# Attention by pairs of heads with a feature-major result, and the squares of the residual moved from GpSimd to ScalarE and VectorE

## The chip, the cores and the metric

The kernel runs on one core of a Trainium2 chip. The metric is the device time of one execution in microseconds (us). Engines: PE is TensorE (matrix products; PEld its weight loads), DVE is VectorE, ACT is ScalarE, POOL is GpSimd, SP issues the loads.

## What is computed

A chain of blocks on 256 tokens of 1024 features, in f32: layer 0 (half a feed-forward, a Mamba-2 mixer, half a feed-forward, shared keys and values), layer 1 (half a feed-forward, windowed attention on the shared keys and values, half a feed-forward), then a block with two mixers and a layer of 16,384 experts. The change touches the attention of layer 1 and the norm at the entry of each block. From the reference:

```python
def rmsnorm(x, g):
    xf = x.astype(jnp.float32)
    y = xf * lax.rsqrt(jnp.mean(xf * xf, axis=-1, keepdims=True) + EPS)
    return (y * g.astype(jnp.float32)).astype(x.dtype)

# sliding_window_attention, one block of 128 queries; 16 query heads of 64, 2 key heads
        s = jnp.einsum('bqkrd,bskd->bkrqs', qk, kk).astype(jnp.float32) * scale + bias
        valid = in_window & ((bi > 0) | (kj >= blk))
        s = jnp.where(valid, s, -jnp.inf)
        m = jnp.maximum(jnp.max(s, axis=-1, keepdims=True), sink)
        p = jnp.exp(s - m)
        denom = jnp.sum(p, axis=-1, keepdims=True) + jnp.exp(sink - m)
        return jnp.einsum('bkrqs,bskd->bqkrd', (p / denom).astype(vk.dtype), vk)
```

## The kernel before

The residual `h` lies feature-major: 8 parts of 128 features by 256 tokens. Every large product is made of three: weights and inputs are each split into a high part that PE takes at full rate and a rest, and `mm3` (lines 153 to 155) adds low weight by high input, high by low and high by high. Weights arrive in groups of 8 blocks of 128 x 128; for each group ACT makes the high part (line 93) and DVE the rest (line 99).

Each block begins with `norm_in`: the gain is multiplied in and the part split, on ACT (line 181) and DVE (line 182), while `norm_sum` (lines 206 to 210) squares and adds the 8 parts on POOL; the scale per token, made from the sum, is put in after the products. The expert layer (`peer`) calls `norm_sum` itself and splits the parts into `uhi` and `ulo`. Eight entries of blocks do this: four feed-forward layers, Mamba, attention, the two mixers together, experts. In four of them the residual is updated part by part some 8 us apart (line 319, behind a feed-forward layer); in three, two parts at a time (lines 261 and 501); the first reads the input.

Attention: `project` makes the queries of four heads (two groups of weights each), their squares by POOL, the sums per head by PE (line 674) and the factors on DVE. `attn_head` handles one head: scores by PE (lines 609 and 610, the head's 64 features on one half of the partitions), scale, bias and maximum on DVE (613 to 616), the exponential on ACT (619), three transposes by PE (623), a copy by ACT (628), and three products with the values (630 to 632) that leave 64 columns per head in a token-major bank `po`. After eight heads `tail` divides by the denominator (708), transposes back to feature-major (716) and splits for the output projection (719 and 720), which runs in two halves of four pairs (`proj_half`, line 261 adds it to `h`). Projections, output projection and heads are woven step by step, and a scheduler that works from estimates sets the final order on each engine. All of PSUM is one pool of 8 banks (`K.bank`). `K.warm` issues dummy products of zeros.

Of the kernel before, what the change touches and what calls it, by code (L numbers as in the profile page):

```python
# [7 lines left out]
F32 = mybir.dt.float32  # L8
# [4 lines left out]
AF = mybir.ActivationFunctionType  # L13
# [4 lines left out]
T = 256  # L18
# [30 lines left out]
class Ctx:  # L49
# [145 lines left out]

    def bcast(self, rt, st, c, n, out):

        self.nc.tensor.matmul(out, rt[:, st, c:c + 1].to_broadcast([128, n]), self.ident, start=True, stop=True)

    def norm_sum(self, h):  # L200

        nc = self.nc
        acc = self.tmp.tile([128, T], F32, name="ssq", tag="ssq")
        for k in range(KD):
            if k == 0:
                nc.gpsimd.tensor_mul(acc, h[:, k], h[:, k])
            else:
                s = self.tmp.tile([128, T], F32, name="sq", tag="sq", bufs=2)
                nc.gpsimd.tensor_mul(s, h[:, k], h[:, k])
                nc.gpsimd.tensor_add(acc, acc, s)  # L210
            yield acc

    def norm_in(self, h, g):

        nc = self.nc
        hi = self.xp.tile([128, KD, T], F32R, name="xhi", tag="xhi")
        lo = self.xp.tile([128, KD, T], F32R, name="xlo", tag="xlo")
        for k, acc in enumerate(self.norm_sum(h)):
            self.split_x(h, g, hi, lo, k)

        def scale(between=None, tok=False):
            rt = self.rs_tok(acc, self.ones[:, 0:1], 1, 1.0 / 1024, EPS, "n")
            if tok:
                return rt
            if between is not None:
                between()
            ps = self.bank()
            for st in range(2):
                self.bcast(rt, st, 0, 128, ps[:, st * 128:(st + 1) * 128])
            rs = self.tmp.tile([128, T], F32, name="rs", tag="rs", bufs=2)  # L230
            nc.scalar.activation(rs, ps[:, :T], AF.Copy)
            return rs, rt

        return hi, lo, scale
# [408 lines left out]
def attention(K, h, P, kv, w_q, w_o, bias, pool):  # L643
# [8 lines left out]
    den = pool.tile([128, 16, 2], F32, name="den")  # L652
    sc = pool.tile([128, 16, 2], F32, name="qsc")
    u = pool.tile([128, 16, 2], F32, name="qu")
    otok = pool.tile([128, 2, 1024], F32, name="otok")
    ohi = pool.tile([128, 8, T], F32R, name="ohi")
    olo = pool.tile([128, 8, T], F32R, name="olo")
    blk = K.stream(w_q)
# [24 lines left out]
            V.tensor_scalar(sv[:, st], sv[:, st], rt[:, st], 0.125, OP.mult, OP.mult)  # L683
        scaled.append(m)

    def head(hd):
        kvh, p0, c = hd // 8, 64 * (hd % 2), (hd % 8) * 64
        while hd // 4 not in scaled:
            yield
        if hd % 8 == 0:  # L690
            po[kvh] = [K.bank("po") for _ in range(2)]
        s = pool.tile([128, 384], F32, name="as", tag="as", bufs=4)
        sT = pool.tile([128, 384], F32, name="asT", tag="asT", bufs=3)
        yield from attn_head(K, s, qT[p0:p0 + 64, hd // 2], kd[p0:p0 + 64, kvh], vtok[:, :, kvh * 64:kvh * 64 + 64],
                             sc[:, hd], (bias[:, hd, 128:256], bias[:, hd]), nsink[:, hd:hd + 1], nm[:, hd], den[:, hd],
                             [p[:, c:c + 64] for p in po[kvh]], sT, hd % 4 < 0)
        if hd % 8 == 7:
            tails.append(tail(kvh))

    def tail(g):  # L700
        gs = slice(8 * g, 8 * g + 8)
        V.tensor_tensor(u[:, gs], nm[:, gs], nsink[:, gs].unsqueeze(2).to_broadcast([128, 8, 2]), OP.subtract)
        A.activation(u[:, gs], u[:, gs], AF.Exp)
        yield
        V.tensor_add(den[:, gs], den[:, gs], u[:, gs])
        V.reciprocal(den[:, gs], den[:, gs])
        for st in range(2):
            V.tensor_tensor(otok[:, st, g * 512:(g + 1) * 512].rearrange("p (a b) -> p a b", b=64),
                            po[g][st].rearrange("p (a b) -> p a b", b=64),
                            den[:, gs, st].unsqueeze(2).to_broadcast([128, 8, 64]), OP.mult)  # L710
        for _ in range(1):
            yield
        for st in range(2):
            ps = K.bank()
            for i in range(4):
                TE.transpose(ps[:, i * 128:(i + 1) * 128], otok[:, st, (4 * g + i) * 128:(4 * g + i + 1) * 128], K.ident)
            dst = (slice(None), slice(g * 4, g * 4 + 4), slice(st * 128, st * 128 + 128))
            pr = ps.rearrange("p (a b) -> p a b", b=128)
            A.activation(ohi[dst], pr, AF.Copy)
            V.tensor_sub(olo[dst], pr, ohi[dst].bitcast(F32))  # L720
            yield
        done.append(g)

    def heads():
        for _ in weave((head(hd) for hd in range(16)), 1):
            if tails and next(tails[0], tails) is tails:
                tails.pop(0)
            yield
        while tails:
            if next(tails[0], tails) is tails:  # L730
                tails.pop(0)
            yield

    def fill():
        for m in range(1, 4):
# [4 lines left out]
                yield  # L740
            yield from K.proj_half(blk, g, ohi[:, 4 * g:4 * g + 4], olo[:, 4 * g:4 * g + 4], h)

    scaled, tails, done, po = [], [], [], {}
    p0 = project(0)
    for _ in range(2):
        next(p0)
    rt = scale(tok=True)
    run((p0, 1), (fill(), 1), (heads(), 1))


EM05 = float(np.exp(-0.5))
# [1210 lines left out]
```

## Time and profile before

| | |
|---|---|
| median of 3 runs | 2160.61 us (2148.82 to 2167.58) |
| the profiled execution | 2161.79 us |
| its span in the trace | 2160.0 us |
| mean granted clock of PE | 0.982 |
| busy: PE, DVE, ACT, POOL | 97%, 72%, 50%, 14% |

The span is what the trace covers, 1.8 us less than the execution's own time. Busy PE time is not PE at its peak: products overlap, so the cost of one is read from the starts of two that follow each other, and the same products take twice the time where the granted clock stands at its lower level. The attention stage lies at about 804 to 904 us of the span, its heads from 816.8; the entries of the blocks lie at 0, 204, 404, 606, 804, 897, 1101 and 1308 us.

### The profile page before, as it was taken

To read this page: it belongs to the slowest core of one execution; us is meant where nothing else is said; L and a number is where in the kernel's file an instruction comes from. 1 tells how busy PE (TensorE), PEld (TensorE's weight loads), DVE (VectorE), ACT (ScalarE), POOL (GpSimd) and SP (SyncE) were. 2 spreads that over 40 slices of the span, in tenths; PEclk is the share of its full clock that TensorE was granted. 3 is DMA by queue.
4 is the path that set the end of the run, shared out by engine and by line. 5 is a ranking of instruction groups with operands and counts; after the bars stand their busy time and mean duration, and the time that the engine had idled before them with its cause. 6 is when DMAs were issued, how large, how long until landed. Compare 5 with 4: busy or idle time off the path is not lost. (4 is left out here: it accounts for less than half of the span.)

```text
span 2160.0 us, 40955 instructions
## 1 busy us (share of the span) xinstructions
PE 2103.4 (97%) x16522; PEld 1981.3 (92%) x16522; DVE 1556.5 (72%) x2862; ACT 1070.0 (50%) x1810; POOL 295.3 (14%) x246
## 2 busy tenths in 40 slices
PE   8999999999999999999998898999999999999999
PEld 8999998999999998899987778999999998888887
DVE  6665978776576656576569778997788886656565
ACT  4444678454454444454443445553444444454544
POOL 2002000200100020200154316751000000000000
PEclk9999999999999997899999999999999999999999
DMA  6555443676555552355542206542444444555554
GB/s 210 186 187 178 157 149 98 174 203 205 181 181 179 188 181 79 118 186 186 186 147 74 94 23 218 167 168 85 159 161 158 157 158 168 191 188 192 187 193 148
DMA packets 98282, 348.16 MB, mean 161 GB/s; under 512 B 11083, under 2 KB 13996, under 8 KB 97836
## 3 DMA queue, kind: packets, MB, share of 16 engines
q1 hardware_dynamic: 98092, 345.54, 48.4%
q8 instruction: 130, 2.13, 0.4%
q14 instruction: 60, 0.49, 0.1%
HBM read 344.05 MB, written 1.44 MB: 160 GB/s over the span
## 5 line engine op out<-in xcount | busy, mean ns | idle before, releaser
L99 DVE TENSOR_TENSOR wlo<-wraw,whi 128x1024 fp32r<-128x1024 f32 x597 | 743.0, 1246 | 304.6 <-ACT whi L93 302.5
L93 ACT ACTIVATE whi<-wraw 128x1024 fp32r<-128x1024 f32 x644 | 677.1, 1053 | 402.0 <-PE ps L155 218.7
L153 PE MATMUL ps<-xhi,wlo 128*128 128x256 f32 x1960 | 561.8, 287 | 15.8 <-DVE wlo L124 7.7
L154 PE MATMUL ps<-xlo,whi 128*128 128x256 f32 x1960 | 557.0, 284 | 2.1 <-DVE xlo L182 1.4
L155 PE MATMUL ps<-xhi,whi 128*128 128x256 f32 x1960 | 555.3, 284 | 0.0
L153 PEld LDWEIGHTS ps<-xhi,wlo 128*128 128x128 f32 x1960 | 375.4, 192 | 23.5 <-DVE wlo L124 7.6
L154 PEld LDWEIGHTS ps<-xlo,whi 128*128 128x128 f32 x1960 | 375.5, 192 | 4.8 <-DVE xlo L182 4.7
L155 PEld LDWEIGHTS ps<-xhi,whi 128*128 128x128 f32 x1960 | 375.3, 191 | 0.3
L153 PE MATMUL ps<-phi,wlo 128*128 128x256 f32 x1024 | 294.5, 288 | 10.0 <-ACT phi L1489 4.1
L154 PE MATMUL ps<-plo,whi 128*128 128x256 f32 x1024 | 288.9, 282 | 0.7 <-DVE plo L1490 0.7
L155 PE MATMUL ps<-phi,whi 128*128 128x256 f32 x1024 | 287.9, 281 | 0.0
L153 PEld LDWEIGHTS ps<-phi,wlo 128*128 128x128 f32 x1024 | 194.6, 190 | 11.8 <-ACT phi L1489 4.3
L1668 PE MATMUL pacc<-whi,cl 128*128 128x512 f32 x512 | 203.8, 398 | 1.5 <-DVE cl L1660 1.5
L1670 PE MATMUL pacc<-whi,ch 128*128 128x512 f32 x512 | 200.6, 392 | 0.0
L1669 PE MATMUL pacc<-wlo,ch 128*128 128x512 f32 x512 | 199.4, 390 | 0.0
L155 PE MATMUL ps<-ghi,whi 128*128 128x256 f32 x704 | 198.2, 282 | 0.0
L153 PE MATMUL ps<-ghi,wlo 128*128 128x256 f32 x704 | 198.1, 281 | 0.0
L154 PE MATMUL ps<-glo,whi 128*128 128x256 f32 x704 | 197.4, 280 | 0.0
L154 PEld LDWEIGHTS ps<-plo,whi 128*128 128x128 f32 x1024 | 194.4, 190 | 0.9 <-DVE plo L1490 0.9
L155 PEld LDWEIGHTS ps<-phi,whi 128*128 128x128 f32 x1024 | 193.8, 189 | 0.0
L154 PEld LDWEIGHTS ps<-glo,whi 128*128 128x128 f32 x704 | 133.2, 189 | 0.0
L153 PEld LDWEIGHTS ps<-ghi,wlo 128*128 128x128 f32 x704 | 132.4, 188 | 0.0
(531 smaller groups left out, 3273.8 us busy)
## 6 DMA issues: line engine op xcount, KB each, us to landing
wraw<-in_w SPq DMA_DIRECT2D x262, 512.0 KB, 3.6
wraw<-in_p_u SPq DMA_DIRECT2D x128, 512.0 KB, 3.6
wraw<-in_p_v SPq DMA_DIRECT2D x128, 512.0 KB, 3.5
wraw<-in_m_win SPq DMA_DIRECT2D x40, 512.0 KB, 4.0
wraw<-in_x_win SPq DMA_DIRECT2D x20, 512.0 KB, 3.6
wraw<-in_m_wout SPq DMA_DIRECT2D x16, 512.0 KB, 3.8
wraw<-in_p_wpq SPq DMA_DIRECT2D x16, 512.0 KB, 4.3
wraw<-in_a_wq SPq DMA_DIRECT2D x8, 512.0 KB, 3.3
```

Of the source, the lines that this page charges most:

```text
L93: nc.scalar.activation(hi, w, AF.Copy)
L99: (nc.vector if lo_eng == "dve" else nc.gpsimd).tensor_sub(lo, w, hi.bitcast(F32))
L153: nc.tensor.matmul(ps, wl, xh, start=first, stop=False)
L154: nc.tensor.matmul(ps, wh, xl, start=False, stop=False)
L155: nc.tensor.matmul(ps, wh, xh, start=False, stop=last)
L1668: TE.matmul(o, cl[:, t], vh[:, f], start=False, stop=False)
L1669: TE.matmul(o, ch[:, t], vl[:, f], start=False, stop=False)
L1670: TE.matmul(o, ch[:, t], vh[:, f], start=False, stop=last)
```

## The change

`norm_sum`: each square is made by ACT, each sum by DVE; POOL takes no part. In `norm_in` the part is now split before its square is asked for; in `peer` the square still comes first.

Attention: a generator `pair` takes two heads that share a query part, on opposite halves of the partitions. Scores go to two banks, in turns of the two halves; maxima and the sink's exponential are taken for both heads at once; the second head's transposes are copied by DVE. The values are now the stationary operand and the probabilities move, 256 and 128 columns at a time, so the result is feature-major, a head on each half of the partitions of one bank. The denominator's reciprocal is spread over that bank's other half by a product with the identity (`bcast`), copied out by ACT, multiplied in by DVE, and the pair is split at once. `otok`, the tails and their transposes go. The output projection's first half may begin after the fourth pair. Pairs are woven two steps apart, heads were one.

```diff
     def bcast(self, rt, st, c, n, out):
-        self.nc.tensor.matmul(out, rt[:, st, c:c + 1].to_broadcast([128, n]), self.ident, start=True, stop=True)
+        r = rt if st is None else rt[:, st]
+        self.nc.tensor.matmul(out, r[:, c:c + 1].to_broadcast([128, n]), self.ident, start=True, stop=True)
...
             if k == 0:
-                nc.gpsimd.tensor_mul(acc, h[:, k], h[:, k])
+                nc.scalar.activation(acc, h[:, k], AF.Square)
             else:
                 s = self.tmp.tile([128, T], F32, name="sq", tag="sq", bufs=2)
-                nc.gpsimd.tensor_mul(s, h[:, k], h[:, k])
-                nc.gpsimd.tensor_add(acc, acc, s)
+                nc.scalar.activation(s, h[:, k], AF.Square)
+                nc.vector.tensor_add(acc, acc, s)
...
-        for k, acc in enumerate(self.norm_sum(h)):
+        sums = self.norm_sum(h)
+        for k in range(KD):
             self.split_x(h, g, hi, lo, k)
+            acc = next(sums)
...
+    def pair(n):
+        kvh, gs, halves = n // 4, slice(2 * n, 2 * n + 2), (slice(0, 64), slice(64, 128))
+        while n // 2 not in scaled:
+            yield
+        s = pool.tile([128, 2, 384], F32, name="as", tag="as", bufs=3)
+        sT = pool.tile([128, 2, 384], F32, name="asT", tag="asT", bufs=2)
+        pl = [K.bank() for _ in range(2)]
+        K.warm(pl[0], 1)
+        for e, p in enumerate(halves):
+            TE.matmul(pl[e][:, 0:128], qT[p, n, 0:128], kd[p, kvh, 0:128], start=True, stop=True)
+        for e, p in enumerate(halves):
+            TE.matmul(pl[e][:, 128:384], qT[p, n, 128:256], kd[p, kvh], start=True, stop=True)
+        yield
+        for e in range(2):
+            hd = 2 * n + e
+            for st, (a, b) in enumerate(SPANS):
+                V.scalar_tensor_tensor(s[:, e, a:b], pl[e][:, a:b], sc[:, hd, st:st + 1], bias[:, hd, 128 - 128 * st:], OP.mult, OP.add)
+        for st, (a, b) in enumerate(SPANS):
+            V.tensor_reduce(nm[:, gs, st], s[:, :, a:b], AX.X, OP.max, negate=True)
+        V.tensor_tensor(nm[:, gs], nm[:, gs], nsink[:, gs].unsqueeze(2).to_broadcast([128, 2, 2]), OP.min)
+        yield
...
+                A.activation(s[:, e, a:b], s[:, e, a:b], AF.Exp, bias=nm[:, hd, st:st + 1], accum_out=den[:, hd, st:st + 1])
+        V.tensor_tensor(u[:, gs], nm[:, gs], nsink[:, gs].unsqueeze(2).to_broadcast([128, 2, 2]), OP.subtract)
         A.activation(u[:, gs], u[:, gs], AF.Exp)
         yield
+        pt = [K.bank() for _ in range(2)]
+        for e in range(2):
+            for b in range(3):
+                TE.transpose(pt[e][:, b * 128:(b + 1) * 128], s[:, e, b * 128:(b + 1) * 128], K.ident)
         V.tensor_add(den[:, gs], den[:, gs], u[:, gs])
         V.reciprocal(den[:, gs], den[:, gs])
+        yield
+        A.activation(sT[:, 0], pt[0][:, :384], AF.Copy)
+        V.tensor_copy(sT[:, 1], pt[1][:, :384])
+        yield
+        po = K.bank()
+        v = vtok[:, :, kvh * 64:kvh * 64 + 64]
+        for e, p in enumerate(halves):
+            TE.matmul(po[p, 0:256], v[:, 0], sT[:, e, 0:256], start=True, stop=False)
+        for e, p in enumerate(halves):
+            TE.matmul(po[p, 128:256], v[:, 1], sT[:, e, 256:384], start=False, stop=True)
         for st in range(2):
...
+            for e, p in enumerate(halves):
+                K.bcast(den[:, 2 * n + e], None, st, 64, po[p, 256 + st * 128:384 + st * 128])
+        yield
+        o = pool.tile([128, T], F32, name="ao", tag="ao", bufs=2)
+        A.activation(o, po[:, 256:512], AF.Copy)
+        V.tensor_tensor(o, o, po[:, 0:256], OP.mult)
+        yield
+        A.activation(ohi[:, n], o, AF.Copy)
+        V.tensor_sub(olo[:, n], o, ohi[:, n].bitcast(F32))
+        if n % 4 == 3:
+            done.append(n // 4)
...
-    run((p0, 1), (fill(), 1), (heads(), 1))
+    run((p0, 1), (fill(), 1), (weave((pair(n) for n in range(8)), 2), 1))
```

PE, behind the sums of squares (`qsq`) of the last projected queries, where the products with the values (`po<-vtok,asT`, now `ps<-asT,vtok`), transposes (`ps<-cst,as`) and scores (`ps<-kd,qT`) follow each other. Before, one head's turn:

```order
L630 MATMUL po<-vtok,asT 128x64
L631 MATMUL po<-vtok,asT 128x64
L632 MATMUL po<-vtok,asT 128x64
L623 MATMUL ps<-cst,as 128x128 x3
L609 MATMUL ps<-kd,qT 128x128
L610 MATMUL ps<-kd,qT 128x256
```

PE at the same place in the changed kernel, one pair's turn (`ps<-cst,den` is the broadcast, `zero` the dummy product):

```order
L730 MATMUL ps<-asT,vtok 64x256 x2
L732 MATMUL ps<-asT,vtok 64x128 x2
L199 MATMUL ps<-cst,den 64x128 x4
L720 MATMUL ps<-cst,as 128x128 x6
L77 LDWEIGHTS zero
L77 MATMUL ps<-zero 128x256
L698 MATMUL ps<-kd,qT 128x128 x2
L700 MATMUL ps<-kd,qT 128x256 x2
```

Six products of 64 columns for two heads became four of 256 and 128 columns, with four broadcasts behind them that wait for DVE's reciprocal.

DVE at the entry of the second feed-forward layer of layer 1, behind attention, before (line 261 updates `h`, two parts at a time):

```order
L261 TENSOR_TENSOR h<-h,ps 128x512
L99 TENSOR_TENSOR wlo<-wraw,whi 128x1024
L182 SCALAR_TENSOR_TENSOR xlo<-h,gains,xhi 128x256 x2
L261 TENSOR_TENSOR h<-h,ps 128x512
L99 TENSOR_TENSOR wlo<-wraw,whi 128x1024
L182 SCALAR_TENSOR_TENSOR xlo<-h,gains,xhi 128x256 x2
L99 TENSOR_TENSOR wlo<-wraw,whi 128x1024 x3
```

DVE at the same place after (line 264 is the former 261, line 211 the sum of squares):

```order
L99 TENSOR_TENSOR wlo<-wraw,whi 128x1024
L182 SCALAR_TENSOR_TENSOR xlo<-h,gains,xhi 128x256
L264 TENSOR_TENSOR h<-h,ps 128x512
L211 TENSOR_TENSOR ssq<-ssq,sq 128x256
L182 SCALAR_TENSOR_TENSOR xlo<-h,gains,xhi 128x256
L211 TENSOR_TENSOR ssq<-ssq,sq 128x256
L182 SCALAR_TENSOR_TENSOR xlo<-h,gains,xhi 128x256
L211 TENSOR_TENSOR ssq<-ssq,sq 128x256
L182 SCALAR_TENSOR_TENSOR xlo<-h,gains,xhi 128x256
L211 TENSOR_TENSOR ssq<-ssq,sq 128x256
L99 TENSOR_TENSOR wlo<-wraw,whi 128x1024 x4
```

The weights' split (`wlo`) stood between the last residual update and the last splits; now sums stand between these, and the weights' split stands ahead of the last update.

DVE at the entry of the expert layer, before:

```order
L261 TENSOR_TENSOR h<-h,ps 128x512
L99 TENSOR_TENSOR wlo<-wraw,whi 128x1024
L261 TENSOR_TENSOR h<-h,ps 128x512
L182 SCALAR_TENSOR_TENSOR ulo<-h,pa,uhi 128x256 x8
L99 TENSOR_TENSOR wlo<-wraw,whi 128x1024 x2
```

DVE there in the changed kernel:

```order
L211 TENSOR_TENSOR ssq<-ssq,sq 128x256 x2
L264 TENSOR_TENSOR h<-h,ps 128x512
L182 SCALAR_TENSOR_TENSOR ulo<-h,pa,uhi 128x256 x6
L211 TENSOR_TENSOR ssq<-ssq,sq 128x256
L182 SCALAR_TENSOR_TENSOR ulo<-h,pa,uhi 128x256
L211 TENSOR_TENSOR ssq<-ssq,sq 128x256
L182 SCALAR_TENSOR_TENSOR ulo<-h,pa,uhi 128x256
L99 TENSOR_TENSOR wlo<-wraw,whi 128x1024 x2
```

Two sums came in between the last splits; the other five stand ahead of the last residual update.

## Rows read from the trace of the kernel before

**Rows 1.** The page: busy PE, and the granted clock in 40 slices.

```profile
PE 2103.4 (97%) x16522; PEld 1981.3 (92%) x16522; DVE 1556.5 (72%) x2862; ACT 1070.0 (50%) x1810; POOL 295.3 (14%) x246
...
PEclk9999999999999997899999999999999999999999
```

**Rows 2.** Windows, attention's heads and output projection: engines' busy time, clock, DMA.

```profile
816.80:877.70 60.90, 60.17 (x322) 50.04 (x322) 36.23 (x137) 30.20 (x90) 3.12 (x3) 0.71 0.15 53
877.70:904.00 26.30, 26.30 (x217) 26.21 (x216) 18.64 (x25) 11.57 (x18) 6.46 (x7) 0.97 0.49 175
```

**Rows 3.** Windows of 20 us inside the attention stage, same columns.

```profile
840.00:860.00 20.00, 20.00 (x115) 16.54 (x114) 11.72 (x48) 8.80 (x25) 1.04 (x1) 0.76 0.16 53
860.00:880.00 20.00, 19.57 (x81) 16.17 (x81) 7.40 (x25) 7.40 (x26) 0.00 (x0) 0.51 0.08 27
```

**Rows 4.** Timeline of PE: start, duration, line, tiles, count; 848 to 850.

```profile
848.17 0.49 PE L609 MATMUL ps<-kd,qT 64*128 64x128 f32 x2
...
849.02 0.44 PE L630 MATMUL po<-vtok,asT 128*128 128x64 f32 x2
...
849.74 0.50 PE L623 MATMUL ps<-cst,as 128*128 128x128 f32 x3
850.16 0.37 PE L609 MATMUL ps<-kd,qT 64*128 64x128 f32 x1
```

**Rows 5.** Timeline of PE, the same work from 857 to 861.

```profile
857.46 0.79 PE L609 MATMUL ps<-kd,qT 64*128 64x128 f32 x2
...
861.15 0.58 PE L609 MATMUL ps<-kd,qT 64*128 64x128 f32 x1
```

**Rows 6.** Line 182 on DVE: least, median and longest ns, then first and last start.

```profile
L182 DVE SCALAR_TENSOR_TENSOR xlo<-h,gains,xhi x56: 474/831/966, 5.1 to 1098.0; 128x256 fp32r<-128x256 f32 x56
L182 DVE SCALAR_TENSOR_TENSOR kvlo<-h,gains,kvhi x8: 471/474/476, 606.9 to 610.8; 128x256 fp32r<-128x256 f32 x8
```

**Rows 7.** Waits of PE from 890 to 920: total us, times, longest.

```profile
PE ps L153 <- DVE wlo L99: 0.8, 1, 0.8
PE ps L153 <- ACT xhi L181: 0.6, 1, 0.6
```

**Rows 8.** Timeline of PE at the first three heads.

```profile
816.80 0.50 PE L609 MATMUL ps<-kd,qT 64*128 64x128 f32 x4
...
817.56 0.38 PE L609 MATMUL ps<-kd,qT 64*128 64x128 f32 x2
```

**Rows 9.** Timeline of PE in Mamba, a pair of heads.

```profile
330.13 0.66 PE L487 MATMUL ps<-sc,xtok 128*64 128x256 f32 x4
...
330.93 0.50 PE L470 MATMUL ps<-ahl,identr 64*128 64x256 f32 x2
```

**Rows 10.** Timeline of PE in the mixers, broadcasts on halves.

```profile
1136.92 1.09 PE L198 MATMUL ps<-cst,kks 128*64 128x128 f32 x16
1137.94 0.39 PE L153 MATMUL ps<-xhi,wlo 128*128 128x256 f32 x1
```

**Rows 11.** Line 77, the dummy products of the mixers, columns as in rows 6.

```profile
L77 PE MATMUL ps<-zero x36: 269/274/286, 1202.8 to 1272.5; 128*128 128x256 bf16 x36
```

**Rows 12.** A window in the mixers, columns as in rows 2.

```profile
1220.00:1240.00 20.00, 19.00 (x246) 15.86 (x242) 15.98 (x38) 8.68 (x16) 5.95 (x4) 1.00 0.25 80
```

**Rows 13.** DVE's groups from 816.8 to 904: busy us, mean ns, idle before.

```profile
L613 DVE SCALAR_TENSOR_TENSOR as<-ps,qsc,t5b 128x256 f32<-128x256 f32 x16 | 7.6, 477 | 0.0
...
L720 DVE TENSOR_TENSOR olo<-ps,ohi 128x512 fp32r<-128x512 f32 x4 | 2.8, 690 | 7.1 <-ACT ohi L719 7.0
L708 DVE TENSOR_TENSOR otok<-po,den 128x512 f32<-128x512 f32 x4 | 2.6, 683 | 0.0
```

**Rows 14.** Groups of the whole span: a square by ACT, a two-operand step of DVE.

```profile
L492 ACT ACTIVATE ysq<-yv 128x256 f32<-128x256 f32 x16 | 6.6, 416 | 6.4 <-DVE yv L491 2.1 <-DVE qnt L171 1.8 <-DVE qny L172 1.8
...
L525 DVE TENSOR_TENSOR ylo<-yv,yhi 128x256 fp32r<-128x256 f32 x16 | 6.2, 419 | 0.3 <-ACT yhi L524 0.2
```

**Rows 15.** Timeline of DVE at the entry of the expert layer.

```profile
1308.44 6.23 DVE L182 SCALAR_TENSOR_TENSOR ulo<-h,pa,uhi 128x256 fp32r<-128x256 f32 x8
```

More of the change, by code (lines that the diff above doesn't have):

```diff
@@ L654, in attention @@
     u = pool.tile([128, 16, 2], F32, name="qu")
-    otok = pool.tile([128, 2, 1024], F32, name="otok")
     ohi = pool.tile([128, 8, T], F32R, name="ohi")
@@ L684, in project @@
         scaled.append(m)
-    def head(hd):
-        kvh, p0, c = hd // 8, 64 * (hd % 2), (hd % 8) * 64
-        while hd // 4 not in scaled:
+    def pair(n):
+        kvh, gs, halves = n // 4, slice(2 * n, 2 * n + 2), (slice(0, 64), slice(64, 128))
+        while n // 2 not in scaled:
             yield
[L690 to L698, printed above, removed]
@@ L700, in tail @@
-    def tail(g):
-        gs = slice(8 * g, 8 * g + 8)
-        V.tensor_tensor(u[:, gs], nm[:, gs], nsink[:, gs].unsqueeze(2).to_broadcast([128, 8, 2]), OP.subtract)
+        s = pool.tile([128, 2, 384], F32, name="as", tag="as", bufs=3)
[4 more added lines that the diff above has]
+            TE.matmul(pl[e][:, 0:128], qT[p, n, 0:128], kd[p, kvh, 0:128], start=True, stop=True)
@@ L703, in tail @@
+        V.tensor_tensor(nm[:, gs], nm[:, gs], nsink[:, gs].unsqueeze(2).to_broadcast([128, 2, 2]), OP.min)
+        yield
+        for e in range(2):
+            hd = 2 * n + e
+            for st, (a, b) in enumerate(SPANS):
+                A.activation(s[:, e, a:b], s[:, e, a:b], AF.Exp, bias=nm[:, hd, st:st + 1], accum_out=den[:, hd, st:st + 1])
+        V.tensor_tensor(u[:, gs], nm[:, gs], nsink[:, gs].unsqueeze(2).to_broadcast([128, 2, 2]), OP.subtract)
         A.activation(u[:, gs], u[:, gs], AF.Exp)
@@ L704, in tail @@
         yield
+        pt = [K.bank() for _ in range(2)]
+        for e in range(2):
+            for b in range(3):
+                TE.transpose(pt[e][:, b * 128:(b + 1) * 128], s[:, e, b * 128:(b + 1) * 128], K.ident)
         V.tensor_add(den[:, gs], den[:, gs], u[:, gs])
         V.reciprocal(den[:, gs], den[:, gs])
-        for st in range(2):
-            V.tensor_tensor(otok[:, st, g * 512:(g + 1) * 512].rearrange("p (a b) -> p a b", b=64),
-                            po[g][st].rearrange("p (a b) -> p a b", b=64),
-                            den[:, gs, st].unsqueeze(2).to_broadcast([128, 8, 64]), OP.mult)
@@ L711, in tail @@
[L711 to L732, printed above, removed]
+        yield
[4 more added lines that the diff above has]
+        v = vtok[:, :, kvh * 64:kvh * 64 + 64]
@@ L741, in fill @@
             yield from K.proj_half(blk, g, ohi[:, 4 * g:4 * g + 4], olo[:, 4 * g:4 * g + 4], h)
-    scaled, tails, done, po = [], [], [], {}
+    scaled, done = [], []
     p0 = project(0)
```

## The prediction

> **What bounds the kernel now.** I read the page first: the granted clock stands at full in most of its 40 slices, and TensorE (PE) is busy nearly everywhere, so time is won where PE has less to do, waits, or runs at the lower clock [rows 1]. Then I asked for stretches. The attention stage, from the first score product of head 0 to the last product of the output projection, lasts 60.9 + 26.3 = 87.2 us. PE is busy in all of it, but at a mean granted clock of 0.71 and 0.97 [rows 2]. The worst part is 860 to 880 us at 0.51, that is nearly all at the lower level of 1.2 GHz [rows 3]. So the stage loses 60.9 x 0.29 + 26.3 x 0.03 = 18.5 us to the clock, and its PE work at full clock is 87.2 - 18.5 = 68.7 us. Third, the timeline of PE gives the price of one head at full clock, 848.17 to 850.16: scores 0.85, probabilities by values 0.72, three transposes 0.42, in all 1.99 us [rows 4]. The same head at the lower clock takes 861.15 - 857.46 = 3.69 us [rows 5]. Fourth, the eight entries of stages, where the residual is squared, summed and split: DVE's splitting step (line 182) takes a median of 831 ns while GpSimd (POOL) squares and adds, and 474 ns where it is done for the shared keys with no squares beside it [rows 6]. PE waits there a little: 1.4 us at the entry of the fourth feed-forward layer [rows 7].
>
> **The change, attention on PE.** An f32 matmul stands as two instructions in the trace, a transpose as one. Removed: 16 heads x 1.99 = 31.8, and the 16 transposes of the tails at 0.42 / 3 = 0.14, 2.2; together 34.0 us. Added for each of 8 pairs:
> Scores: eight instructions, the two heads on opposite halves of the rows, issued in turn. The trace has this already once, by chance of the order: the first two heads together took 817.56 - 816.80 = 0.76 us, not 1.70 [rows 8].
> Probabilities by values, now with the values stationary and 256 and 128 columns moving, each head on one half of the output partitions: the state-space layer's pair has just these shapes and took 330.93 - 330.13 = 0.80 us, where two heads now take 1.44 [rows 9].
> Broadcast of the reciprocals, four matmuls, eight instructions: 16 of the same shape took 1.02 us in the mixers, so 0.51 [rows 10].
> Six transposes: 0.84 [rows 4]. One dummy product: at most its whole duration, 0.27 [rows 11].
> Sum 0.76 + 0.80 + 0.51 + 0.84 + 0.27 = 3.18, times 8 = 25.4 us. So 8.6 us of PE work go, all of it on the path, since PE is hardly ever idle there [rows 2]: 60.1 us are left at full clock.
>
> **The clock and the waits.** Added to these 60.1 us is what is lost to the lower clock and to waits: 18.5 us now, and nothing at best. Between the head at 848, still at full clock, and the one at 857, at the lower [rows 4, 5], PE had only score products of single heads, 64-column products, transposes and the sums of squares of a projection; it stayed low while that went on, and the output projection ran at 0.97 [rows 2]. In the new order every such run is broken by the paired products of 256 columns and a dummy product. The mixers are the nearest rows: from 1220 to 1240 PE has only small paired products with dummy ones between them, and the clock is 1.00 [rows 12]. That is nearer to the new work than single heads are, so I take most of the loss as gone. But new waits come: pair n's broadcast stands in PE's queue behind the reciprocal of DVE, with the next pair's transposes and scores queued behind it, and the output copy, product and two splits follow before line 155 may use pair 3 or 7. I take 8 us of loss, a little under half of today's; the ends are 0 and 18.5. So 60.1 + 8 = 68 us, a gain of 87.2 - 68 = 19 us (8.6 to 27).
>
> **DVE in attention.** It is busy 36.23 + 18.64 = 54.9 us of the 87.2 [rows 2]. The eight 512-column steps of the tails go, 4 x 0.683 + 4 x 0.690 = 5.5 us [rows 13]. Each pair gets one copy of 384 columns, between the 0.48 of 256 and the 0.68 of 512 columns [rows 13], say 0.58, and two steps of 256 columns at 0.42 [rows 14], 1.42 us, or 11.4 for all; joined reductions and the small steps about cancel. So 54.9 - 5.5 + 11.4 = 61 us: as much as PE. It hides behind PE only if it hardly ever waits.
>
> **Squares by ACT, sums by DVE.** Each entry puts eight squares of about 0.42 on ACT and seven sums of about 0.42 on DVE [rows 14], and takes 15 steps off POOL. In the four entries behind a feed-forward layer seven of eight parts lie under the down projection, and only the last is seen: the split is faster by 0.36, the sum of squares is asked for later on PE. I take 0.3 us each, 1.2. At the two entries behind a pair-wise residual update (feed-forward layers two and four) DVE is full. Per two parts it now does two splits of 0.47 and two sums of 0.42, 1.78 us, in place of two splits of 0.83, 1.66 us: even. What is won is the weights' split, which now stands ahead of the last parts, and on which PE waits 0.8 us [rows 7]: 0.8 each, 1.6. At the entry of the expert layer POOL's six early squares become early squares and sums on ACT and DVE; behind the last residual update DVE has then 8 splits and 2 sums, 8 x 0.47 + 2 x 0.42 = 4.6 us, in place of 6.23 [rows 15]: 1.6. At the kernel's start ACT and DVE are the bound of the first products, and both get more: -0.5, with -2 as an end. Together 1.2 + 1.6 + 1.6 - 0.5 = 4 us; the ends are -2, if sums behind squares hold DVE up as POOL did, and +8, if all waits of these entries go.
>
> **Sum.** The profiled execution took 2161.8 us, the median of the three runs is 2160.6 (2148.8 to 2167.6), so it stands for them. 2161.8 - 19 - 4 = 2139 us.
>
> **Rivals.** *DVE sets the pace.* DVE's 61 us are not below PE's 60.1; in the second part of the stage, the denser for it, it is busy 18.64 of 26.3, 71% [rows 2]. At 80% it needs 76 us: gain 11, 2161.8 - 11 - 4 = 2147. For it speaks that copies, products and splits all moved into the pairs; against it that each wait of DVE on PE now seen in the stage shrinks with PE's work.
> The Trainium skill, TensorEngine Tiling (Array Packing), section PSUM Bottleneck, says the same: packing small products speeds up TensorE but not the emptying of PSUM, which may become the bottleneck. The trace so far neither shows nor excludes it, since nothing in this stage is packed but by chance; by that rule 2147 would be the time.
> *The clock falls as before.* 18.5 us are lost all the same: 60.1 + 18.5 = 78.6, gain 8.6, 2149. For it: the product of squares and the transposes still stand between the pairs.
> *The halves don't run together.* Then scores cost 1.70, values 1.60 and broadcasts 1.02 a pair, 2.2 us more, 18 in all: 86 us, gain 1, 2157. The three rows above speak against it.
> *Slower: PE waits at every broadcast.* If the reciprocal comes late for each pair, PE stands still before it, and the whole first part runs at the lower clock: its work of 60.9 x 0.71 - 8.6 = 35 us becomes 70, with a wait of 1 us a pair 78, and with 26 us behind it 104, against 87.2: 2161.8 + 17 - 4 = 2175. It turns to a loss from the point where clock and waits cost over 27 + 4 us. Against it: the transposes of another pair stand in the order between the exponentials and the broadcast.
>
> **How the numbers follow.** The forecast, with its own range 2125 to 2144, 0.54; DVE's pace 0.20; the clock as before 0.12; no running together 0.06; slower 0.08. Eight in ten then lie from 2125 to 2155; the lower end is 4 us of loss and 8 of gain at the entries, with some 4 us of spread between runs, the upper one the halves not together. The bound of what a measurement here can tell from no change is 1%, that is below 2139.0 or above 2182. Two thirds of the forecast lie under it (0.36), and with the larger gains at the entries some of DVE's pace and of the clock as before (0.09): faster by over 1% 0.45; slower, most of the last rival, 0.06; within 1% the rest, 0.49.
>
> **What would show it.** In the changed kernel: from the first score product to the last of the output projection about 68 us at a granted clock above 0.9; a pair's scores in about 0.76 and its values in 0.80 us; line 182 at a median near 0.47 us; the eight splits at the expert layer's entry with their last two sums within 5 us. Wrong would be PE waiting on reciprocals or copies of DVE for more than 10 us, a clock of 0.5 between the pairs, or a first product that starts more than 2 us later.

## The result and the profile after

| | before | changed |
|---|---|---|
| median of 4 runs, us | 2162.55 (2148.82 to 2167.58) | 2127.11 (2122.25 to 2128.37) |
| ratio | | 0.9838, 95% interval 0.981 to 0.9866 |
| span of the profiled execution, us | 2160.0 | 2126.6 |

The changed kernel is 35 us faster, where 23 were forecast (19 in attention, 4 at the entries of the blocks). The page of the changed kernel answers to [rows 1]: GpSimd (POOL) has shrunk by 114 us, and the slices of the granted clock that stood at 7 and 8 are gone.

```profile
PE 2075.0 (98%) x16546; PEld 1957.8 (92%) x16546; DVE 1556.2 (73%) x2928; ACT 1089.8 (51%) x1884; POOL 181.4 (9%) x126
...
PEclk9999999999999999999999999999999999999999
```

Both traces hold the same 12,384 instructions of the three-product multiplications in nearly the same order. The start of the n-th in one trace against the other therefore tells where time was won: up to the first score product 5.4 us, in the attention stage 23.6, behind it 4.4, together 33.4. Of the first 5.4, 1.8 lie in the Mamba layer, some 60 us behind its entry, where the change touches nothing: there the profiled execution of the kernel before ran 3.4 us (265.1 to 268.5) at a clock of 0.50.

The attention stage, from the first score product to the end of the output projection (windows view of the changed kernel: length, then busy us of PE, PEld, DVE, ACT, POOL, granted clock, DMA share, GB/s; the first row ends with the last product of the query projections, the second with the first of the output projection, the fourth is the whole):

```profile
811.39:834.25 22.86, 22.86 (x206) 20.07 (x206) 21.87 (x82) 16.59 (x50) 2.08 (x2) 1.00 0.26 87
834.25:844.05 9.80, 9.80 (x96) 7.14 (x94) 9.12 (x32) 7.63 (x27) 1.04 (x1) 1.00 0.23 72
844.05:874.98 30.93, 29.84 (x265) 27.55 (x264) 26.11 (x61) 19.67 (x48) 0.00 (x0) 1.00 0.48 168
811.39:874.98 63.59, 62.50 (x561) 54.76 (x561) 57.09 (x174) 43.90 (x124) 3.12 (x3) 1.00 0.36 124
```

It takes 63.6 us at full clock, where it took 87.2 at 0.71 and 0.97 [rows 2]. One pair's turn in the timeline of PE (start, us, line), which answers to [rows 4], with the scores of another pair that answer to [rows 8]:

```profile
817.36 0.49 PE L698 MATMUL ps<-kd,qT 64*128 64x128 f32 x4
817.69 0.60 PE L700 MATMUL ps<-kd,qT 64*128 64x256 f32 x4
818.22 0.38 PE L153 MATMUL ps<-xhi,wlo 128*128 128x256 f32 x1
...
834.46 0.65 PE L730 MATMUL ps<-asT,vtok 128*64 128x256 f32 x4
834.94 0.39 PE L732 MATMUL ps<-asT,vtok 128*64 128x128 f32 x4
835.16 0.61 PE L199 MATMUL ps<-cst,den 128*64 128x128 f32 x8
835.70 0.88 PE L720 MATMUL ps<-cst,as 128*128 128x128 f32 x6
836.41 0.27 PE L77 MATMUL ps<-zero 128*128 128x256 bf16 x1
836.61 0.49 PE L698 MATMUL ps<-kd,qT 64*128 64x128 f32 x4
```

From start to start: scores 0.86, values 0.70, broadcasts 0.54, transposes 0.71, dummy 0.20, in all 3.01 us a pair. No product and no weight load waits at a broadcast; PE's products wait only for the exponentials (waits of PE from 811 to 875: total us, times, longest):

```profile
PE ps L720 <- ACT as L713: 1.1, 2, 0.9
```

At the entries, VectorE's (DVE's) splits have lost their slow form (line 182, least/median/longest ns; answers to [rows 6]), and at the expert layer the splits and the last sums end 3.9 us after the first split starts (timeline of DVE; answers to [rows 15]):

```profile
L182 DVE SCALAR_TENSOR_TENSOR xlo<-h,gains,xhi x56: 469/479/489, 4.8 to 1065.2; 128x256 fp32r<-128x256 f32 x56
```

```profile
1277.65 2.46 DVE L182 SCALAR_TENSOR_TENSOR ulo<-h,pa,uhi 128x256 fp32r<-128x256 f32 x6
1280.03 0.42 DVE L211 TENSOR_TENSOR ssq<-ssq,sq 128x256 f32<-128x256 f32 x1
1280.37 0.48 DVE L182 SCALAR_TENSOR_TENSOR ulo<-h,pa,uhi 128x256 fp32r<-128x256 f32 x1
1280.76 0.42 DVE L211 TENSOR_TENSOR ssq<-ssq,sq 128x256 f32<-128x256 f32 x1
1281.10 0.48 DVE L182 SCALAR_TENSOR_TENSOR ulo<-h,pa,uhi 128x256 fp32r<-128x256 f32 x1
```

### The profile page after: what moved, and what is told of

The parts are those of the page before. It is cut to its first block, busy times and chain, and to the rows that moved or that the text cites. A ratio compares the mean times of both kernels' runs of the same rounds, so it can differ in the third digit from the quotient of the medians.

```text
span 2126.6 us, 40988 instructions
## 1 busy us (share of the span) xinstructions
PE 2075.0 (98%) x16546; PEld 1957.8 (92%) x16546; DVE 1556.2 (73%) x2928; ACT 1089.8 (51%) x1884; POOL 181.4 (9%) x126
## 5 line engine op out<-in xcount | busy, mean ns | idle before, releaser
L153 PE MATMUL ps<-xhi,wlo 128*128 128x256 f32 x1960 | 557.8, 285 | 12.7 <-DVE wlo L124 6.8
L99 POOL TENSOR_TENSOR wlo<-wraw,whi 128x1024 fp32r<-128x1024 f32 (+1 forms) x47 | 115.8, 2469 | 312.0 <-ACT whi L93 299.5
```

The lines of the kernel that those rows point to most:

```text
L99: (nc.vector if lo_eng == "dve" else nc.gpsimd).tensor_sub(lo, w, hi.bitcast(F32))
L153: nc.tensor.matmul(ps, wl, xh, start=first, stop=False)
```

## The experiments

All ratios stand beside runs of the kernel before on the same chip. Its medians there: 2160.8 us for attention alone, the norm alone, no dummies, and a dummy per head; 2159.7 for GpSimd's sums in the new order, heads in series, the copy made twice, and the squares of the queries on ScalarE; 2159.6 for both copies on ScalarE, scores in pairs, and dummies in the mixers; 2161.1 for parted scores.

### The two parts, each alone

Attention by pairs with the norm of the kernel before:

```diff
-                nc.scalar.activation(acc, h[:, k], AF.Square)
+                nc.gpsimd.tensor_mul(acc, h[:, k], h[:, k])
...
-        sums = self.norm_sum(h)
-        for k in range(KD):
+        for k, acc in enumerate(self.norm_sum(h)):
             self.split_x(h, g, hi, lo, k)
-            acc = next(sums)
```

> Attention by pairs alone; squares and sums of the norm on GpSimd as before, with the square asked for ahead of the split. Theory (the two parts add up): the attention stage, from the first score product to the last of the output projection, takes about 64 us as in the changed kernel, line 182 goes back to a median near 0.83 us, and the entries lose what they had won: 2162.6 - 23.6 = 2139 us. Rival (the entries were not faster because of the norm, but because of what attention leaves behind): 2127 us, with line 182 slow and no longer waits. Second rival (GpSimd's squares hold up VectorE in the stages next to attention, more than at the other entries): 2145 us.

Measured: 2137.2 us (2136.6 to 2138.7), ratio 0.9897 (0.9876 to 0.9917). The window of the stage and line 182 of this kernel:

```profile
816.40:880.02 63.62, 62.54 (x561) 54.78 (x561) 57.10 (x171) 41.49 (x117) 9.49 (x10) 1.00 0.36 122
```

```profile
L182 DVE SCALAR_TENSOR_TENSOR xlo<-h,gains,xhi x56: 473/830/964, 4.8 to 1074.2; 128x256 fp32r<-128x256 f32 x56
```

The theory held to 2 us. Against the changed kernel this run lacks the norm edit alone, so the starts of the same products give the norm's share place by place: at the second feed-forward layer 4.2 us, at the third 0.5, at attention 0.3, at the fourth feed-forward layer 4.0, in the mixers -0.8, at the expert layer 2.2, together 10.3 (the chips of the two runs differ; by the ratios to the kernel before, 0.9897 and 0.9838, it would be 12.7). At the second feed-forward layer PE waits as before (waits from 410 to 425), and then runs 3.4 us at the lower level of the clock (windows, same columns as above; the second row is the entry of the fourth feed-forward layer); in the changed kernel it does neither:

```profile
PE ps L153 <- DVE wlo L99: 0.9, 1, 0.9
PE ps L153 <- ACT xhi L181: 0.6, 1, 0.6
PE ps L154 <- DVE xlo L182: 0.4, 1, 0.4
```

```profile
416.00:419.40 3.40, 3.40 (x17) 3.40 (x18) 1.22 (x1) 1.06 (x1) 1.69 (x3) 0.51 0.29 105
887.00:890.40 3.40, 3.40 (x18) 3.40 (x18) 1.32 (x1) 1.06 (x1) 1.33 (x2) 0.50 0.36 63
```

The norm alone, with the attention of the kernel before:

```diff
-                nc.gpsimd.tensor_mul(acc, h[:, k], h[:, k])
+                nc.scalar.activation(acc, h[:, k], AF.Square)
...
-                nc.gpsimd.tensor_mul(s, h[:, k], h[:, k])
-                nc.gpsimd.tensor_add(acc, acc, s)
+                nc.scalar.activation(s, h[:, k], AF.Square)
+                nc.vector.tensor_add(acc, acc, s)
```

> Squares by ScalarE and sums by VectorE alone; attention head by head as before. Theory: line 182 at a median of 0.48 us, the eight splits at the expert layer's entry with their last sums within 5 us, waits of TensorE at the entries shorter, attention stage 87 us as before: 2162.6 - 10 = 2153 us. Rival (nothing of it is on the path): 2162 us within the spread. Second rival (the clock intervals beside the entries move with them): the entries differ from the changed kernel by steps of some 1.7 us.

Measured: 2146.8 us (2137.3 to 2155.8), ratio 0.9934 (0.9916 to 0.9953). That is 14 us, with an interval of 10 to 18, more than the 8 that the theory's 2153 us stood for. With the 23.6 of attention alone it makes 37.6, against 35.4 for both, so the parts add up within their spread. Not all 14 need be the norm's: this run's ten executions spread over 18.5 us, with a mean clock from 0.978 to 0.989, and in the profiled one the attention stage, which the edit does not touch, took 84.0 us at a clock of 0.82 in place of 87.2. So the norm is worth 10 to 14 us.

Then the norm edit itself was parted: the split asked for first, as in the changed kernel, but squares and sums on GpSimd.

```diff
-                nc.scalar.activation(s, h[:, k], AF.Square)
-                nc.vector.tensor_add(acc, acc, s)
+                nc.gpsimd.tensor_mul(s, h[:, k], h[:, k])
+                nc.gpsimd.tensor_add(acc, acc, s)
```

> The changed kernel with squares and sums on GpSimd as before, but the split still asked for ahead of the square. It parts the two halves of the norm edit. Theory (GpSimd's squares and sums slow down VectorE's split while they run): line 182 near 0.83 us again, 2135 to 2138 us, as with the old norm altogether (2137.2). Rival (what counts is that the split comes first): 2127 to 2129 us, line 182 mostly near 0.48 us.

Measured: 2138.4 us (2135.5 to 2146.6), ratio 0.9929 (0.9903 to 0.9956), with line 182 slow again:

```profile
L182 DVE SCALAR_TENSOR_TENSOR xlo<-h,gains,xhi x56: 474/832/964, 4.8 to 1071.3; 128x256 fp32r<-128x256 f32 x56
```

So the engine counts, not the order: with GpSimd's squares and sums beside it the same split takes 1.7 times as long (832 against 479 ns). The Trainium skill, GPSIMD Engine Reference, section Specifications, says that GpSimd's SBUF interfaces are shared with VectorE and that VectorE's instructions with two inputs from SBUF contend for them; the split of line 182 has two such inputs, and the trace agrees with its 832 against 479 ns.

### The dummies

```diff
         pl = [K.bank() for _ in range(2)]
-        K.warm(pl[0], 1)
```

> The changed kernel without the dummy product of each pair. Theory (the paired products of 256 columns keep TensorE's clock up, the dummies are small change): clock near 1.00 in the attention stage, 8 x 0.2 = 1.6 us less, 2125 to 2126 us. Rival (the dummies hold the clock): stretches at half the clock between the pairs again, half of the old loss or more, so 9 to 18 us more: 2136 to 2144 us.

Measured: 2126.2 us (2124.1 to 2128.0), ratio 0.985 (0.9829 to 0.987); the stage:

```profile
810.57:873.93 63.36, 61.98 (x553) 54.50 (x553) 57.16 (x175) 44.11 (x124) 3.12 (x3) 1.00 0.36 125
```

The clock stays up without them, and taking them away wins 0.2 us of the stage, not the 1.6 that they last; the medians (2126.2 and 2127.1) do not differ clear of their spread. The other way round, one dummy ahead of each single head in the kernel before:

```diff
     ps = K.bank()
+    if cap is not None:
+        K.warm(ps, 1)
     TE.matmul(ps[:, 0:128], q[:, 0:128], k[:, 0:128], start=True, stop=True)
```

> The kernel before, head by head, with one dummy product ahead of each head's scores in the attention of layer 1: 16 in all, at 0.2 us. Theory (single heads are too thin: half of the array's rows, 64 columns): the mean clock of the stage rises a little over 0.71 but stays under 0.85, and the 3.4 us of dummies about eat what it gives: 2160 us, between 2156 and 2166. Rival (the dummies hold the clock): the stage at a clock of 0.95 or more, 18.5 - 3.4 = 15 us less: 2147 us.

Measured: 2164.0 us (2152.0 to 2172.2), ratio 1.0009 (0.9983 to 1.0035): no gain by the median. But the ten executions fall into two groups. Four took 2152 to 2155 us at a mean clock of 0.983 to 0.986, all below the fastest of the 19 executions of the kernel before beside them (2155.9); six took 2163 to 2172 us at 0.976 to 0.980. The profiled one is the fastest of the four, and shows the whole stage at a clock of 0.94, nearly the rival's 0.95; its first row is the piece between the last product of the query projections and the first of the output projection. So a dummy per head can hold the clock in the old order, and by the times did so in four executions of ten.

```profile
847.41:867.68 20.27, 19.82 (x133) 14.54 (x131) 13.25 (x50) 10.52 (x33) 1.04 (x1) 1.00 0.10 33
815.28:894.67 79.39, 78.73 (x552) 68.31 (x552) 54.38 (x161) 42.01 (x108) 9.89 (x10) 0.94 0.29 99
```

### Turns, and scores in pairs

The changed kernel with the two heads of a pair one after the other (likewise for the values and the broadcasts):

```diff
         for e, p in enumerate(halves):
             TE.matmul(pl[e][:, 0:128], qT[p, n, 0:128], kd[p, kvh, 0:128], start=True, stop=True)
-        for e, p in enumerate(halves):
             TE.matmul(pl[e][:, 128:384], qT[p, n, 128:256], kd[p, kvh], start=True, stop=True)
```

> The changed kernel with the two heads of a pair one after the other: both score products of the first head, then both of the second; the same for the products with the values and the broadcasts. The same work, the same halves, only the turns between them are gone. Theory (products on opposite halves run together only when they follow each other in turns): scores near 1.7 us a pair, values 1.4 to 1.6, broadcasts near 1.0, some 2 us more a pair, 16 us in all, less what TensorE waited anyway: 2138 to 2145 us, the clock still near 1.00. Rival (the turns don't matter, the halves overlap in any order or the gain is fewer products): 2127 us, scores 0.85 us.

Measured: 2128.1 us (2126.7 to 2129.0), ratio 0.9877 (0.9822 to 0.9932). The theory fell. In PE's program the four score products of a pair now stand head by head, and yet in the timeline of PE all instructions of the 128-column products (line 698) of both heads still start ahead of all those of 256 columns (line 699), and the scores take 0.86 us as before:

```profile
817.62 0.50 PE L698 MATMUL ps<-kd,qT 64*128 64x128 f32 x4
817.94 0.61 PE L699 MATMUL ps<-kd,qT 64*128 64x256 f32 x4
818.48 0.38 PE L153 MATMUL ps<-xhi,wlo 128*128 128x256 f32 x1
```

The second head's first product did not wait for the first head's second: the halves run side by side also when the work of one head stands behind the other's; turns are not needed. The kernel before had shown it already: there heads 0 and 1, the pair of [rows 8] that took 0.76 us, stand in PE's program one behind the other, not in turns.

The kernel before with nothing but the scores of two heads asked for together; values, tails and the norm as they were (this also lets two heads advance in one step of the weave):

```diff
-    def head(hd):
+    def two(n):
...
+        for ps, p in zip(pl, halves):
+            TE.matmul(ps[:, 0:128], qT[p, n, 0:128], kd[p, kvh, 0:128], start=True, stop=True)
+        for ps, p in zip(pl, halves):
+            TE.matmul(ps[:, 128:384], qT[p, n, 128:256], kd[p, kvh], start=True, stop=True)
+        yield
+        yield from weave((rest(hd, s, ps, v, [x[:, (hd % 8) * 64:(hd % 8) * 64 + 64] for x in po[kvh]]) for hd, s, ps in zip(hs, ss, pl)), 1)
```

> The kernel before, norm on GpSimd, values as the moving operand, 64 columns a head, tails at the end: all as before; only the scores of two heads are asked for one behind the other, without a dummy. TensorE has 8 x (1.70 - 0.86) = 6.7 us less to do. Theory (the new products with the values, the broadcasts and the lack of 64-column products keep the clock up, the scores are a part of it): the clock of the stage rises to between 0.75 and 0.9, 2144 to 2154 us. Rival 1 (the paired scores alone hold the clock): near 1.00, 2138 to 2143 us, as attention by pairs alone has 2137. Rival 2 (what counts is the order of steps, not the products): 2160 us.

Measured: 2140.3 us (2135.9 to 2144.2), ratio 0.9915 (0.9877 to 0.9953). This alone gives 19 of the 24 us of attention by pairs, as the first rival had it, at a clock of 0.95. Its stage, cut at the last product of the query projections and the first of the output projection, and below it the same middle piece of the kernel before:

```profile
814.25:842.39 28.14, 27.19 (x209) 25.20 (x208) 21.69 (x87) 17.32 (x50) 2.08 (x2) 0.88 0.29 95
842.39:855.63 13.24, 11.93 (x106) 10.66 (x104) 11.86 (x48) 10.23 (x33) 1.04 (x1) 1.00 0.01 2
...
814.25:883.30 69.05, 66.15 (x538) 62.48 (x538) 54.43 (x162) 41.45 (x107) 9.46 (x10) 0.95 0.33 113
```

```profile
847.01:875.02 28.01, 28.01 (x125) 21.94 (x124) 13.90 (x51) 11.38 (x35) 1.04 (x1) 0.59 0.07 25
```

That run changed two things: the scores side by side, and the order of the heads' steps. A full-width product of zeros, 2 columns, between the two heads' scores takes away the first:

```diff
         for ps, p in zip(pl, halves):
+            if ps is pl[1]:
+                TE.matmul(ps[:, 0:2], K.zero[:, 0:1].to_broadcast([128, 128]), K.zero, start=True, stop=True)
             TE.matmul(ps[:, 0:128], qT[p, n, 0:128], kd[p, kvh, 0:128], start=True, stop=True)
-        for ps, p in zip(pl, halves):
             TE.matmul(ps[:, 128:384], qT[p, n, 128:256], kd[p, kvh], start=True, stop=True)
```

> The kernel with scores in pairs and all else as before (it had taken 2140 us, its attention stage 69 us), with one more thing: the second head's scores are asked for behind the first head's, and a product of zeros over the whole array, 2 columns wide, stands between the two heads, so that they can't run side by side. The order of all other steps stays nearly the same. That run had changed two things at once, the scores side by side and the order of the heads' steps; this takes the first away and leaves the second. Theory (side by side is what shortens the stage and keeps the clock up): 8 x 0.85 = 6.8 us more work, and the clock falls as before, 8 to 15 us more: 2155 to 2162 us, clock of the first part under 0.85. Rival (the order of the steps keeps the clock up, side by side saves only its own time): 2146 to 2148 us, stage 76 us, clock of the first part 0.9 or more.

Measured: 2143.7 us (2139.4 to 2148.4), ratio 0.9924 (0.9901 to 0.9946).

```profile
815.19:843.07 27.88, 27.32 (x215) 23.70 (x215) 22.65 (x91) 17.89 (x51) 2.08 (x2) 1.00 0.29 96
843.07:857.28 14.21, 12.89 (x108) 11.18 (x106) 11.92 (x43) 9.75 (x31) 1.05 (x1) 1.00 0.01 2
...
815.19:884.56 69.37, 67.33 (x546) 61.60 (x545) 55.57 (x162) 41.50 (x107) 9.59 (x10) 1.00 0.33 112
```

The clock is 1.00 with the scores parted: the rival held for the clock, not for its price (it had a stage of 76 us; 69.4 were measured). Five of the six executions have a mean clock of 0.988 or 0.989 and one 0.983, the eleven of the kernel before beside them 0.976 to 0.984, so it is not the profiled one alone. Two limits: two pairs are asked for in a row, so the second head of one still ran beside the first of the next (the timeline of PE has such a group of four at 838.43), and only about half of the side by side was gone; and the eight products of zeros that part the heads are small dummies themselves. The time is 3.4 us above the run with scores in pairs, which is not clear of their spread.

### VectorE's load

The second head's copy made twice, and, in another kernel, both copies on ScalarE:

```diff
         V.tensor_copy(sT[:, 1], pt[1][:, :384])
+        V.tensor_copy(sT[:, 1], pt[1][:, :384])
```

```diff
-        V.tensor_copy(sT[:, 1], pt[1][:, :384])
+        A.activation(sT[:, 1], pt[1][:, :384], AF.Copy)
```

> The changed kernel with VectorE's copy of the second head's transposes made twice, 8 x 0.55 = 4.4 us more work on VectorE, nothing else. Rival of the prediction (VectorE sets the pace in attention, where it is busy 57 of 63.5 us): about 4.4 us more, 2131 to 2132 us. Theory (TensorE sets it, VectorE has some slack left at nearly every step): less than 1.5 us more, 2127 to 2128.5 us; the attention stage of 63.5 us grows by under 1.5.

> The changed kernel with both transposes' copies of a pair on ScalarE: VectorE has 8 x 0.55 = 4.4 us less to do in attention, ScalarE 3.9 us more (it is busy 44 of 63.5 us). It is the other side of the run that made the copy twice and took 3 us more. If VectorE sets the pace of the stage: 2 to 4 us less, 2123 to 2125 us. If its load only shows where a step is late (theory): within 1.5 us of 2127. If ScalarE's two copies in a row hold the products with the values up: 1 to 3 us more.

Measured: twice, 2130.1 us (2125.0 to 2133.0), ratio 0.988 (0.9824 to 0.9937); on ScalarE, 2123.5 us (2121.7 to 2128.0), ratio 0.9835 (0.9798 to 0.9872). The stage with the copy twice, then with both copies on ScalarE:

```profile
813.06:880.88 67.82, 65.46 (x561) 56.51 (x560) 60.94 (x183) 43.84 (x124) 3.12 (x3) 0.97 0.34 117
```

```profile
813.39:874.71 61.32, 61.32 (x560) 54.50 (x560) 54.47 (x166) 46.01 (x132) 3.12 (x3) 1.00 0.38 129
```

4.4 us of copies more on DVE made the stage 4.2 us longer, 67.8 x 0.03 = 2.0 of them by the clock, and 4.4 us less made it 2.3 us shorter and left PE no idle time. So about half of each microsecond of these copies lies on the path. That is an estimate from one execution of each kernel, of which the one with the copy twice was the slowest of its four, and it goes by the copies' durations: DVE's busy time rose by 3.9 us and fell by only 2.6, since its steps overlap. The theory's bound of 1.5 us was too low, and the rival is half right. Of the gain of 3.6 us in the last run only 2.3 belong to the stage (see the end). It is the fastest kernel of the study by its median; against the changed kernel's 2122 to 2128 that is not clear of the spread.

GpSimd's last work in attention, the squares of the queries, moved to ScalarE as well, without the dummies:

```diff
-        nc.gpsimd.tensor_mul(sq, qT[:, n:n + 2], qT[:, n:n + 2])
+        A.activation(sq, qT[:, n:n + 2], AF.Square)
```

> The changed kernel without the dummy products of the pairs and with the squares of the queries in attention on ScalarE too, so that GpSimd has nothing to do there. Theory (GpSimd's 4.2 us in the stage slow down VectorE, which has little slack): 1 to 3 us less, 2123 to 2126 us. Rival (ScalarE's square is later than GpSimd's and TensorE waits for it at the sums of squares, or VectorE had slack): 2126 to 2128 us.

Measured: 2127.2 us (2126.2 to 2128.4), ratio 0.9877 (0.9822 to 0.9931): nothing, as the rival had it.

### Dummies in the waits of the mixers

```diff
         ps = K.bank()
+        K.warm(ps, 8)
         for j in range(2):
             for st in range(2):
                 for e, p in enumerate(halves):
                     K.bcast(kks, st, 4 * m + 2 * j + e, 64, ps[p, j * T + st * 128:j * T + (st + 1) * 128])
```

(and 6 ahead of each of the sums of squares of the keys, 12 ahead of the transposes)

> The changed kernel with 52 more dummy products in the two mixers, in front of three places where TensorE waits 2.5 to 3.2 us and the clock then falls for 3.4 to 10 us: the sums of squares of the keys, the broadcast of their factors, the transposes of the first mixer's result. Together 11 us of dummies. If they lie in the waits and keep the clock up: some 24 us at the lower level become 12, so 5 to 12 us less, 2115 to 2122 us. If they stand in the way of ready work: up to 11 us more, 2127 to 2138 us.

Measured: 2132.0 us (2130.0 to 2138.8), ratio 0.9876 (0.9837 to 0.9916), 5 us more than the changed kernel. From the last product of the fourth feed-forward layer to the first of the expert layer it took 221.1 us in place of 213.8, with PE busy 8.1 us longer and the mean clock at 0.92 in place of 0.93. So the dummies took time and did not hold the clock up.

## Why the prediction was right, and where its working was not

**PE's work in attention.** Forecast 3.18 us a pair and 8.6 us less in all; measured 3.01, so 34.0 - 8 x 3.01 = 9.9 less. The 34.0 count all 16 heads at the price of single ones, though the first two already ran side by side [rows 8], 1.70 - 0.76 = 0.9 less; so 9.0 less, and 68.7 - 9.0 = 59.7 us left. The three rows taken from elsewhere were good: 0.76, 0.80 and 0.51 against 0.86, 0.70 and 0.54. One reading was wrong: the products of [rows 8] were taken as issued in turn, and they stand head by head.

**Clock and waits.** Forecast 8 us of loss, measured 63.6 - 59.7 = 3.9, with nothing lost to the clock and 1.1 in waits that the trace names; the rest lies in small gaps that were not followed up. So the stage gave 23.6 for 19. The direction was right, the reason only in part. "In the new order every such run is broken by the paired products of 256 columns and a dummy product" named two things: the dummy is not needed in the changed kernel (2126.2 without), and products of 256 columns with stationary values aren't either (scores in pairs with the old values reach 2140). What the changed kernel and the two runs with scores in pairs share is the order. In the kernel before, 28.0 us lie between the last product of the query projections and the first of the output projection, with only heads, their tails and the last sums of squares in them, at a clock of 0.59; that is 16.5 us of work, and 11.5 of the 18.5 us that the stage lost. Where two heads advance in one step, fewer scores are left for this piece (4 heads' instead of 7 with scores in pairs), and it lasts 13.2, 14.2 or, in the changed kernel, 9.8 us at 1.00. The run with parted scores speaks for the order as far as it parts them. The order is not the only thing that can hold the clock: with a dummy per head the same piece in the old order, with the scores of 7 heads, lasted 20.3 us at 1.00 in the profiled execution, and by the times in four of ten. So which property of the piece decides stays open: 14.2 us of such work kept the clock, 16.5 did not, and with dummies among them 20.3 did.

**The norm.** Here the term was mis-sized: 4 us forecast, 10.1 measured beside the new attention (2137.2 - 2127.1) and 14 beside the old, beyond the end of +8. The failed term is the one that begins "What is won is the weights' split" and ends "0.8 each, 1.6", for the two entries behind a pair-wise update. They gave 4.2 and 4.0. Two things were missed. The clock falls behind such a wait, and 3.4 us at half clock cost 1.7 us more (both entries of the run with attention alone show it, the run with GpSimd's sums in the new order at one). The profiled execution of the kernel before bears this out: behind its second feed-forward layer's entry (404 to 425) the clock stood at 1.00, and against it that entry gave 2.7 us. And durations were added where steps overlap: two splits and two sums were put at 1.78 us "in place of two splits of 0.83, 1.66 us: even". In DVE's timeline of the changed kernel splits follow each other every 0.40 us and a sum adds 0.34, so 1.48, against 1.64 from the start of two slow splits to the next step (timeline of DVE before, at the entry behind attention):

```profile
898.04 1.71 DVE L182 SCALAR_TENSOR_TENSOR xlo<-h,gains,xhi 128x256 fp32r<-128x256 f32 x2
899.68 0.67 DVE L261 TENSOR_TENSOR h<-h,ps 128x512 f32<-128x512 f32 x1
```

How much of the 4.2 each of the two made was not parted further. The other terms were near: the expert layer 2.2 for 1.6, the third feed-forward layer and attention 0.8 together for 0.6, the start -0.6 for -0.5, Mamba's entry 0.5 for 0.3, and the mixers' entry 0.9 for 0.3; but 1.7 were lost again inside the mixers, which no term had and which was not followed up.

**The number.** 2127 lies 2 us inside the lower end of the range, 2125. That end stood for 4 us of loss in attention and 8 of gain at the entries; 3.9 and 10 were measured. Both terms fell short in the same direction, so no two errors cancelled, and that the range held was close.

**The rivals.** "DVE sets the pace" is half true: its copies count about one half, while the forecast gave DVE's load no price of its own beside the 8 us of loss. DVE was busy 57.1 us, where 61 were forecast. The Trainium skill, TensorEngine Tiling (Array Packing), section PSUM Bottleneck, advises to empty PSUM with ScalarE and VectorE both. Here the stage with one copy on each engine was 2.3 us longer than with both on ScalarE, which had room (44 of 63.6 us busy), so in these two executions the trace does not agree: the less loaded engine did better than both. "The halves don't run together" and "PE waits at every broadcast" did not come: no wait at line 199 stands in the stage.

## What to carry to other kernels

When a clock falls in one stretch, look at what lies in the stretch and why it lies there: spreading the thin work among dense work by the order of steps may do more than making the thin work denser. Run a kernel several times before you say that something holds the clock: the same kernel can hold it in some executions and not in others. Work on GpSimd beside VectorE should be charged with what it adds to VectorE's own steps. A wait of PE costs more than its length when the clock falls behind it, and a chain of short steps should be priced by the distance of their starts, not by their durations.

## What the runs showed of the hardware

PE does not hold back work for one half of the array until earlier work for the other half has started: the scores of two heads in series took 0.86 us, as in turns. A product over the whole array between them does part them: in the run with parted scores a single head, 837.47 to the product of zeros at 838.32, took 0.85 us by itself.

In the profiled executions the matmuls of the fourth feed-forward layer run at one of two paces, depending on the kernel, at a granted clock of 1.00 in both. In the 40 us from 920 on, the changed kernel has 114 products of line 153, the one with both copies on ScalarE 119 (groups of PE by line: busy us, mean ns, idle before):

```profile
L153 PE MATMUL ps<-xhi,wlo 128*128 128x256 f32 x114 | 31.9, 280 | 0.0
```

```profile
L153 PE MATMUL ps<-xhi,wlo 128*128 128x256 f32 x119 | 32.8, 276 | 0.0
```

The layer is 3.7 us shorter at the faster pace (184.8 against 188.5 us from the end of the output projection), which the kernel with dummies in the mixers has too. The profiled execution with both copies on ScalarE is 5.8 us shorter than that of the changed kernel: 2.0 lost ahead of attention, 2.3 won in the stage, 3.7 here, 1.8 behind it. What sets the pace was not found.
